# Input projection in seven block products, with tokens in three outer parts

## The chip, the cores and the metric

The kernel runs on one core of a Trainium2 chip. The core has a matrix engine (PE, TensorE), three engines for elementwise work (DVE or VectorE, ACT or ScalarE, POOL or GpSimd), a queue engine (SP) that here issues all transfers, and 16 DMA engines. The metric is the device time of one launch in microseconds (us). Before the change it is 1186.73 us, the median of three runs (1184.58 to 1187.98).

## The reference, cut to what matters

One layer with a pooling half and a recurrent half, 2048 prompt tokens and 8 sequences of 8 new tokens (2112 tokens in all), model width 1024. All is float32.

```python
xn = rms_norm(x, norm_pre)
z  = xn @ w_in                      # 1024 -> 4096: v_pool | g_pool | u_lru | g_lru, 1024 columns each
# pooling: causal mean over the last 2/4/8/16 tokens (by channel group) minus the token,
#          then a 256x256 map per group and a scale per channel
y_pool = (mean_window(v_pool) - v_pool) @ pool_w[g] * pool_scale
# recurrence: causal convolution of width 4, two sigmoid gates by 128x128 blocks, a scan
xs = conv4(u_lru) ; r = sigmoid(xs @ wa + ba) ; gi = sigmoid(xs @ wx + bx)
log_a = -8 * r * softplus(-lam) ; a = exp(log_a)
h_t = a_t * h_{t-1} + xs * gi * sqrt(max(-expm1(2*log_a), 1e-12))
merged = concat(y_pool * silu(g_pool), h * silu(g_lru)) @ w_out
y = x + rms_norm(merged, norm_post)  # and the new pool, conv and scan states
```

## The kernel before

Channels lie on the 128 partitions and tokens along the free axis. Each float32 operand of the matrix engine is split into a high and a low float32r half (`split`, L102 to L109: the high half by a copy on ACT, the low half by a subtraction on DVE or POOL), and each product is taken as three matmuls, high x high, high x low and low x high (`z_k`, L302 to L304; `mm3`, L316 to L318; `product`, L978 to L980).

The input projection has 32 blocks of 128 output channels: 8 value blocks and 8 gate blocks of the pooling half, 8 input blocks (u) and 8 gate blocks (lg) of the recurrent half. The tokens are cut into five chunks (four of 426 and one of 408). The split activations of all chunks stay in SBUF (`xn`), and the outer loop runs over blocks: a block's weight is loaded and split once and then meets all five chunks, at 8 x 3 matmuls for a chunk. There are these stages:

- A first stage in an order written out by hand (`tc.manual_schedule`): the first chunk, row norms from a second copy of x (L224), the normalisation of the other chunks (L272, L280, L289), and pooling group 0, with its map by `pool_mm`.
- Pooling groups 1 to 3. For these the map `pool_w` is multiplied into the weight beforehand (`fold_mm`, 12 foldings of 12 matmuls of 256 columns), so that only the last chunk, whose new states need the raw values, still goes through the map. Beside it `w_combos` (L452) forms differences of blocks of `w_out` for the last stage.
- The recurrent half: 40 steps (8 blocks x 5 chunks) in a hand-written order. A step has U's 24 matmuls, the convolution (`conv_stage`: one ACT pass and three DVE passes, L504), the split of its result, the gate matmuls of the step before, the gates (`lru_gates`, L537 to L541), the reciprocal of 1 + tanh on DVE (L1280), the scan (`lru_scan`, L545 to L554) and the product with silu of the gate (`lru_out` on POOL, L566). The decay a is 2/(1 + tanh(lam4 * r)) - 1.
- The output projection, which already takes seven products of 512 x 512 blocks for eight, 56 products of 24 matmuls of 512 columns for 16 x 128 token rows and a short one for the last 64 tokens. It reads the mixed activations back from DRAM (`mixed`) in tiles of 128 tokens.

Every engine works off its own instructions in order. Outside the hand-ordered parts a planner fixes the order when the kernel is built. All transfers are issued by SP in one queue, which stands still while a transfer waits for its tile.

## Time and profile before

| what | value |
|---|---|
| median of three runs | 1186.73 us |
| the profiled execution itself | 1187.95 us |
| its span, first to last instruction | 1186.1 us |
| mean granted TensorE clock | 0.996 |
| DMA moved | 146.93 MB, mean 124 GB/s |
| DVE reciprocals, L1280 | 40, 112.4 us |
| ACT table loads at L1292 and L1272 | 41, 52.6 us |

Busy time of an engine counts the time in which it had an instruction under way. For PE it is not the time at peak rate, since matmuls overlap: the mean of a matmul of 426 columns is 0.36 us, but the next one starts after about half of that. The rate is read from the distance of two starts.

### The profile page before, as it was taken

To read this page: it belongs to the slowest core of one execution; us is meant where nothing else is said; L and a number is where in the kernel's file an instruction comes from. 1 tells how busy PE (TensorE), PEld (TensorE's weight loads), DVE (VectorE), ACT (ScalarE), POOL (GpSimd) and SP (SyncE) were. 2 spreads that over 40 slices of the span, in tenths; PEclk is the share of its full clock that TensorE was granted. 3 is DMA by queue.
4 is the path that set the end of the run, shared out by engine and by line. 5 is a ranking of instruction groups with operands and counts; after the bars stand their busy time and mean duration, and the time that the engine had idled before them with its cause. 6 is when DMAs were issued, how large, how long until landed. Compare 5 with 4: busy or idle time off the path is not lost. (4 is left out here: it accounts for less than half of the span.)

```text
span 1186.1 us, 16264 instructions
## 1 busy us (share of the span) xinstructions
PE 1166.3 (98%) x5794; PEld 1075.2 (91%) x5794; DVE 827.9 (70%) x1201; ACT 551.5 (46%) x1015; POOL 356.4 (30%) x486
## 2 busy tenths in 40 slices
PE   7999999999999999999999999999999999999997
PEld 5899899999999999999999999999968888888886
DVE  4787344443625556888888888889876678888687
ACT  5753311221231136767676676767744333344232
POOL 4145402410431243333334433334310002221242
PEclk9999999999999999999999999999999999999999
DMA  9712533632630110110111111114479866777553
GB/s 341 268 60 62 184 129 115 189 118 75 201 95 30 65 52 26 45 45 33 45 41 54 49 45 45 33 41 120 133 206 259 243 177 189 229 209 232 166 166 142
DMA packets 127904, 146.93 MB, mean 124 GB/s; under 512 B 12432, under 2 KB 87440, under 8 KB 127824
## 3 DMA queue, kind: packets, MB, share of 16 engines
q1 hardware_dynamic: 127824, 145.91, 39.2%
q8 instruction: 45, 0.74, 0.3%
q14 instruction: 35, 0.29, 0.1%
HBM read 106.37 MB, written 39.24 MB: 123 GB/s over the span
## 5 line engine op out<-in xcount | busy, mean ns | idle before, releaser
L504 DVE SCALAR_TENSOR_TENSOR xs<-u,parT,xs 128x426 f32<-128x426 f32 (+1 forms) x120 | 109.2, 910 | 46.9 <-ACT xs L500 30.3
L302 PE MATMUL v<-xh,w 128*128 128x426 f32 (+2 forms) x320 | 116.0, 364 | 6.5 <-ACT w L595 5.6
L971 POOL TENSOR_TENSOR xr<-ac,xr 128x512 f32<-128x512 f32 x28 | 47.6, 1720 | 229.5 <-DMA s2d<-a 110.6
L303 PE MATMUL v<-xl,w 128*128 128x426 f32 (+2 forms) x320 | 115.5, 362 | 0.9 <-DVE xl L611 0.6
L302 PE MATMUL g<-xh,w 128*128 128x426 f32 (+1 forms) x320 | 114.7, 359 | 0.6 <-ACT w L106 0.6
L304 PE MATMUL g<-xh,w 128*128 128x426 f32 (+1 forms) x320 | 114.1, 357 | 0.7 <-POOL w L109 0.7
L304 PE MATMUL v<-xh,w 128*128 128x426 f32 (+2 forms) x320 | 114.1, 360 | 0.4 <-DVE w L109 0.4
L303 PE MATMUL g<-xl,w 128*128 128x426 f32 (+1 forms) x320 | 113.9, 356 | 0.0
L302 PE MATMUL u<-xh,w 128*128 128x426 f32 (+1 forms) x320 | 113.7, 355 | 0.0
L302 PE MATMUL lg<-xh,w 128*128 128x426 f32 (+1 forms) x320 | 113.7, 355 | 0.0
L304 PE MATMUL lg<-xh,w 128*128 128x426 f32 (+1 forms) x320 | 113.5, 355 | 0.0
L304 PE MATMUL u<-xh,w 128*128 128x426 f32 (+1 forms) x320 | 113.4, 354 | 0.0
L303 PE MATMUL lg<-xl,w 128*128 128x426 f32 (+1 forms) x320 | 113.4, 354 | 0.0
L303 PE MATMUL u<-xl,w 128*128 128x426 f32 (+1 forms) x320 | 113.2, 354 | 0.0
L1280 DVE RECIPROCAL rv<-rv 128x426 f32<-128x426 f32 (+1 forms) x40 | 112.4, 2811 | 0.0
L978 PE MATMUL p<-ws,s 128*128 128x512 f32 (+1 forms) x264 | 102.4, 388 | 0.0
L979 PE MATMUL p<-ws,s 128*128 128x512 f32 (+1 forms) x264 | 102.1, 387 | 0.2 <-DVE ws L109 0.2
L980 PE MATMUL p<-ws,s 128*128 128x512 f32 (+1 forms) x264 | 102.0, 387 | 0.1
L980 PE MATMUL p<-ws,a 128*128 128x512 f32 x192 | 75.8, 395 | 1.1 <-DVE a L109 1.1
L978 PE MATMUL p<-ws,a 128*128 128x512 f32 x192 | 75.7, 394 | 0.1
L979 PE MATMUL p<-ws,a 128*128 128x512 f32 x192 | 75.5, 393 | 0.0
L365 DVE TENSOR_TENSOR s<-e 128x440 f32<-128x440 f32 (+3 forms) x40 | 29.1, 728 | 65.4 <-ACT e L336 49.3
(225 smaller groups left out, 2803.2 us busy)
## 6 DMA issues: line engine op xcount, KB each, us to landing
a<-mixed SPq DMA_DIRECT2D x112, 256.0 KB, 4.3
wr<-in_w_in SPq DMA_DIRECT2D x56, 256.0 KB, 3.0
tok<-in_x SPq DMA_DIRECT2D x16, 512.0 KB, 10.2
wo<-in_w_out SPq DMA_DIRECT2D x32, 256.0 KB, 3.7
wtd<-wo SPq DMA_DIRECT2D x32, 256.0 KB, 2.4
w<-wtd SPq DMA_DIRECT2D x32, 256.0 KB, 3.9
xr<-in_x SPq DMA_DIRECT2D x32, 256.0 KB, 3.7
out<-xr SPq DMA_DIRECT2D x30, 256.0 KB, 2.7
```

What stands on the lines that cost most here:

```text
L302: nc.tensor.matmul(out, lhsT=wh, rhs=xh, start=(k == 0), stop=False)
L303: nc.tensor.matmul(out, lhsT=wh, rhs=xl, start=False, stop=False)
L304: nc.tensor.matmul(out, lhsT=wl, rhs=xh, start=False, stop=(k == KT - 1))
L365: nc.vector.tensor_tensor(out=dst[:, first:L], in0=src[:, first:L], in1=src[:, first - sh:L - sh], op=ALU.add)
L504: nc.vector.scalar_tensor_tensor(out=xs, in0=E[:, k:k + n], scalar=col(C_CW + 8 * k, b), in1=xs, op0=ALU.mult, op1=ALU.add)
L971: (eng or nc.vector).tensor_tensor(out=out, in0=a, in1=b, op=op)
L978: nc.tensor.matmul(out, lhsT=ah, rhs=wh, start=start and k == 0, stop=False)
L979: nc.tensor.matmul(out, lhsT=ah, rhs=wl, start=False, stop=False)
L980: nc.tensor.matmul(out, lhsT=al, rhs=wh, start=False, stop=stop and k == KT - 1)
L1280: nc.vector.reciprocal(out=v, in_=v)
```

## The change

The 32 blocks are taken in pairs (16 pairs) and the chunks in pairs too: six chunks of 352 tokens, in three parts of 704. For a pair of blocks, a pair of chunks and the two halves of the 1024 input channels, the 2 x 2 x 2 block product is done with seven products instead of eight (a "quad", `quad_slot`). Each product ("slot") has 4 x 3 matmuls of 352 columns. Four combinations of the four x quarters (T1 to T4) and four of the four weight quarters are formed by additions and split. Five PSUM sums per quad are put together by one ACT copy, one more ACT copy, and five DVE additions that read PSUM.

Tokens are outermost: all 16 pairs are run for part 0, then for part 1, then for part 2. The weight combinations are formed and split in part 0 (for V, G and U of the first pair in part 1, since these three are taken without combinations in part 0), stored to DRAM as split pairs of 512 KB (`wsd`), and loaded from there in parts 1 and 2, one for each slot, seven slots ahead. Of the seven low halves of a quad four are formed on POOL (`LO_POOL`) and three on DVE.

The whole input projection is one hand-ordered sequence. A loop over slots issues the matmuls of one slot, then what became due: evacuations of the slot before, one waiting small matmul group (a pooling map or a gate), delayed transfers, and steps of the generators (`pool_chain`, `conv_chain`, `lru_chain`, `x_chain`, `combos_chain`), as long as the costs written beside their `yield` fit a budget of 1.92 us for each of DVE, ACT and POOL (0.96 us more with a small matmul group).

The folding of `pool_w` into the weight is gone; all four groups of the pooling half go through the map. The reciprocal is gone: ACT gives a first value of 1 + a by Exp and the tanh of half the exponent, and one Newton step for 2/(1 + tanh) mends it, three DVE passes over 704 elements in place of the reciprocal and one pass. Sigmoids are formed with tanh. Elementwise work runs on 704 tokens at a time (728 with the states in the last part). The last stage is kept, with other buffers.

The diff, cut to its core:

```diff
-CW = 426
-CHUNKS = [(s, min(s + CW, T_ALL)) for s in range(0, T_ALL, CW)]
+CW = 352
+MW = 2 * CW
+NM = 3
+CHUNKS = [(s, s + CW) for s in range(0, T_ALL, CW)]
+AHEAD = 7
+SLOT = 1.92
+ORDER = (1, 6, 5, 7, 4, 2, 3)
+XOF = {1: "X11", 6: "T2", 5: "T1", 7: "T3", 4: "T4", 2: "X21", 3: "X22"}
...
+    def quad_product(out, t, name, start, stop, chain=False):
+        for k in range(HK):
+            wh, wl = w_parts(t, k)
+            xh, xl = (xq(name, k, i) for i in range(2))
+            mm(out, wh, xh, start and k == 0, False, chain)
+            mm(out, wh, xl, False, False, chain)
+            mm(out, wl, xh, False, stop and k == HK - 1, chain)
...
+    LO_POOL = (0, 3, 5, 6)
+
+    def w_step(n):
...
+        t = w_tiles[n] = half_tile(f"w{m}{kind}{p}_{i}")
+        if q not in PREP:
+            nc.sync.dma_start(out=flat, in_=wsd[:, key, :])
+            return 0.0, 0.0, 0.0
...
+        elif i == 1:
+            tadd(s1, r["21"], r["22"])
+            tsub(src, s1, r["11"])
+        elif i == 2:
+            tsub(r["21"], r["11"], r["21"])
+        elif i == 4:
+            tsub(s4, r["12"], r["s2"])
...
+        pool = i in LO_POOL
+        split(t[:, 0, :], t[:, 1, :], src, AC, G if pool else V)
+        if m < LM:
+            later(2, lambda: nc.sync.dma_start(out=wsd[:, key, :], in_=flat))
...
+        if pid == 1:
+            quad_product(bank("a"), w, name, True, True)
+
+            def evac():
+                t["tmp"] = t_tile(f"q{n}")
+                AC.copy(out=U(1), in_=t["a"])
+        elif pid == 6:
+            quad_product(bank("b"), w, name, True, True)
+
+            def evac():
+                tadd(U(0), t["b"], U(1))
...
+        elif pid == 7:
+            quad_product(bank("c"), w, name, True, True)
+
+            def evac():
+                tadd(U(1), t["c"], U(0))
+                put_sum(q, 1, 1, t["e"], U(1))
...
+        elif pid == 2:
+            quad_product(t["a"], w, name, False, True, True)
+
+            def evac():
+                AC.copy(out=dst_parts(q, 0, 0)[0][0], in_=t["a"])
...
-        nc.vector.reciprocal(out=v, in_=v)
+        AC.activation(out=gi, in_=gi, func=AF.Identity, bias=ones[:, 0:1])
+        G.tensor_tensor(out=gi, in0=gi, in1=v, op=ALU.mult)
+        AC.activation(out=v, in_=r, func=AF.Exp, scale=nlam[:, b:b + 1], bias=nlam[:, b:b + 1])
+        AC.activation(out=r, in_=r, func=AF.Tanh, scale=lam2[:, b:b + 1], bias=lam2[:, b:b + 1])
+        AC.activation(out=v, in_=v, func=AF.Identity, bias=ones[:, 0:1])
+        V.scalar_tensor_tensor(out=u, in0=r, scalar=1.0, in1=v, op0=ALU.add, op1=ALU.mult)
+        AC.activation(out=r, in_=r, func=AF.Sqrt)
+        V.scalar_tensor_tensor(out=u, in0=u, scalar=-4.0, in1=v, op0=ALU.add, op1=ALU.mult)
+        V.scalar_tensor_tensor(out=r, in0=r, scalar=-0.25, in1=u, op0=ALU.mult, op1=ALU.mult)
+        AC.activation(out=u, in_=u, func=AF.Identity, scale=-0.5, bias=neg1)
+        V.scalar_tensor_tensor(out=gi, in0=r, scalar=0.5e-6, in1=gi, op0=ALU.max, op1=ALU.mult)
+        V.tensor_tensor_scan(out=r, data0=u, data1=gi, initial=0.0 if m == 0 else hh[:, b:b + 1],
+                             op0=ALU.mult, op1=ALU.add)
...
+    def one_slot(pe_fn, used=(0.0, 0.0, 0.0), n_pe=1):
+        length = SLOT
+        outs = [pe_fn()] if pe_fn else []
+        for f in evacs:
+            f()
+        if pe_q and pe_q[0][0] <= now[0]:
+            outs.append(pe_q.pop(0)[1]())
+            length += 0.96
+        evacs.extend(o[0] for o in outs)
+        due_dmas()
+        bud = [min(length - u, length + c - u) for u, c in zip(used, carry)]
+        bud[0] -= sum(o[1] for o in outs)
+        run_gens(bud)
...
+        for n in range(7 * len(QUADS)):
+            qi, i = divmod(n, 7)
+            q = QUADS[qi]
+            if i == 0:
+                while t_free() < {"V": 1}.get(q[2], 3) or (q[2] == "V" and (e_free() < 2 or not sums_done(*q[:2]))):
+                    one_slot(None)
+                quad_begin(q)
...
+            tr = transition(ti) if ti >= 0 else used
+            ws = w_step(n + AHEAD)
+            one_slot(body, [a + b for a, b in zip(tr, ws)])
...
-T_BUFS = 9
+T_BUFS = 14
-E_BUFS = 4
+E_BUFS = 6
+W_BUFS = 8
```

`transition` forms the split x quarters of the next part in the last quad of a part and the first of the next: four quarter combinations and the low halves of T1 to T4 on DVE, the low halves of X11, X21 and X22 on POOL. The order of the quads in a part is V, G, L of the pair before, U, for four channel pairs each, and L of the last pair.

More of the change, by code (lines that the diff above doesn't have):

```diff
@@ L855, in hymba_kernel @@
     ol = late[:, 472:544].rearrange("p (b t) -> p b t", b=NH)
[L856 to L860 removed]
+    hp = sb.tile([P, NH, PB], F32, name="hp")
+    hu = sb.tile([P, NH, CB], F32, name="hu")
+    hh = sb.tile([P, NH], F32, name="hh")
+    lam2 = sb.tile([P, NH], F32, name="lam2")
+    nlam = sb.tile([P, NH], F32, name="nlam")
+    hb = sb.tile([P, 2, NH], F32, name="hb")
@@ new lines, in x_lo, with blocks, w_load_raw @@
+    def x_lo(name, src, eng):
+        hi = q3(name, 0).bitcast(F32)
+        if isinstance(src, list):
+            for o, i, h in zip(parts(q3(name, 1)), parts(src), parts(hi)):
+                tsub(o, i, h, eng)
+        else:
+            tsub(q3(name, 1), src, hi, eng)
+    def blocks(kind, p):
+        return [KINDS[kind] + 2 * p + j for j in range(2)]
+    def w_load_raw(blk, h, tile):
+        nc.sync.dma_start(out=tile, in_=w_in[blk, :, PIECE * h:PIECE * (h + 1)])
+        return tile
@@ L1018, in p1_out @@
     def p1_out(g):
[L1019 removed]
+        nc.scalar.copy(out=acc_new(("m", g)), in_=bank["a", g])
     def p1(g):
```

1759 lines of the change are left out of this document (918 added, 841 removed).

## The prediction

> **What bounds the kernel now.** I read the page's busy times first, then the table of stretches, because one share over the whole span mixes stages with different limits (columns: PE, weight load, DVE, ACT, POOL, each with its count, then clock, DMA share, GB/s).
>
> ```profile
> PE 1166.3 (98%) x5794; PEld 1075.2 (91%) x5794; DVE 827.9 (70%) x1201; ACT 551.5 (46%) x1015; POOL 356.4 (30%) x486
> ...
> 0.00:50.00 50.00, 40.76 (x178) 35.02 (x179) 27.10 (x55) 31.12 (x64) 13.65 (x35) 0.98 0.94 345
> ...
> 437.00:875.00 438.00, 437.69 (x2248) 422.02 (x2248) 363.54 (x402) 303.17 (x508) 162.06 (x266) 1.00 0.19 58
> 875.00:1179.00 304.00, 302.74 (x1325) 244.64 (x1323) 234.28 (x420) 112.15 (x241) 54.36 (x34) 1.00 0.71 207
> ```
>
> PE is occupied from the first matmul to the last; only the start (40.76 of 50 us) and the last 7 us have gaps. So matmul issue bounds the time, and the question is what each matmul costs and which engine follows PE. In the recurrent stage (437 to 875) DVE is at 83%. The price of a matmul is the distance of two starts, in the order of time on PE:
>
> ```profile
> 702.43 0.35 PE L302 MATMUL u<-xh,w 128*128 128x426 f32 x1
> ...
> 706.91 0.36 PE L304 MATMUL u<-xh,w 128*128 128x426 f32 x1
> ...
> 1004.52 0.39 PE L978 MATMUL p<-ws,a 128*128 128x512 f32 x1
> ...
> 1010.06 0.39 PE L978 MATMUL p<-ws,s 128*128 128x512 f32 x1
> ...
> 1173.05 0.28 PE L978 MATMUL p<-ws,s 128*128 128x256 f32 x1
> ...
> 1178.04 0.28 PE L978 MATMUL p<-ws,s 128*128 128x256 f32 x1
> ```
>
> There are 23, 24 and 42 distances between these: 0.195 us for 426 columns, 0.231 for 512, 0.119 for 256. On the line between them 352 columns cost 0.161 and 408 cost 0.185.
>
> **Part 1, matmuls.** The counts are from the code; the rows of before agree with it (two of the twelve input groups, a folding, a gate).
>
> ```profile
> L302 PE MATMUL v<-xh,w 128*128 128x426 f32 (+2 forms) x320 | 116.0, 364 | 6.5 <-ACT w L595 5.6
> L303 PE MATMUL u<-xl,w 128*128 128x426 f32 (+1 forms) x320 | 113.2, 354 | 0.0
> L318 PE MATMUL f<-pw,wtl 128*128 128x256 f32 x48 | 13.7, 286 | 0.2 <-POOL wtl L109 0.2
> L317 PE MATMUL i<-xl,lws 128*128 128x426 f32 x32 | 11.6, 361 | 0.0
> ```
>
> Before: input 32 blocks x 24 x (4 x 0.195 + 0.185) = 741 us; folding 144 x 0.119 = 17; maps 96 at 0.19 = 18; gates 240 x 0.195 = 47; together 823. After: 45 quads x 84 plus six blocks taken plainly, 288, is 4068 x 0.161 = 655; maps 288 x 0.161 = 46; gates 288, 47; together 748. **PE gains 75 us**, and if PE still set the pace the time would be near 1113. The output stage keeps its matmuls, so nothing there.
>
> **Part 2, what DVE and POOL must do beside it.**
>
> ```profile
> L1280 DVE RECIPROCAL rv<-rv 128x426 f32<-128x426 f32 (+1 forms) x40 | 112.4, 2811 | 0.0
> ```
>
> Removed are these 112 us of reciprocals. Added are two DVE passes per recurrent block, five PSUM additions per quad, the weight combinations and the x combinations. Most of the added passes read two tensors from SBUF, and the trace shows what such a pass does beside POOL:
>
> ```profile
> 998.53 3.42 POOL L971 TENSOR_TENSOR xr<-ac,xr 128x512 f32<-128x512 f32 x2 [6.48 <-DVE ac L1111]
> ...
> 999.03 1.78 DVE L109 TENSOR_TENSOR a<-a,a 128x512 fp32r<-128x512 f32 x1
> 1000.81 1.70 DVE L971 TENSOR_TENSOR a<-a,a 128x512 f32<-128x512 f32 x1
> 1002.43 0.68 DVE L109 TENSOR_TENSOR s<-a,s 128x512 fp32r<-128x512 f32 x1
> 1003.03 0.68 DVE L971 TENSOR_TENSOR a<-a,a 128x512 f32<-128x512 f32 x1
> ...
> 73.25 2.10 POOL L289 TENSOR_TENSOR xl<-xr,xh 128x852 fp32r<-128x852 f32 x1 [1.43 <-ACT xh L280]
> ...
> 73.36 2.36 DVE L272 SCALAR_TENSOR_TENSOR xr<-xr,parT,r 128x426 f32<-128x426 f32 x4
> ```
>
> While POOL runs two subtractions, DVE's passes take 1.78 and 1.70 us; right after, the same passes take 0.68 and start 0.60 apart. Two at 0.60 and two of POOL at 1.29 alone make 3.8, and the stretch took 4.0: one after the other. At 73 us DVE's passes have r in PSUM, and four take 2.36 us beside a POOL pass of the usual length: no loss. So DVE's two-SBUF passes and POOL's work share one resource, and their times add. [...]
>
> The prices, each as lowest, median and highest (ns) of a line's passes:
>
> ```profile
> L109 POOL TENSOR_TENSOR wtl<-wt,wth x12: 1284/1288/1300, 124.8 to 343.2; 128x512 fp32r<-128x512 f32 x12
> L566 POOL TENSOR_TENSOR lsg<-lsg,rv x32: 1100/1112/1126, 467.4 to 869.7; 128x426 f32<-128x426 f32 x32
> L289 POOL TENSOR_TENSOR xl<-xr,xh x6: 2025/2068/2385, 73.2 to 91.3; 128x852 fp32r<-128x852 f32 x6
> L548 DVE SCALAR_TENSOR_TENSOR tg<-rv,tg x40: 602/603/609, 465.4 to 873.0; 128x426 f32<-128x426 f32 x32, 128x432 f32<-128x432 f32 x8
> L554 DVE TENSOR_TENSOR_SCAN rv<-rv,hh,tg x32: 1103/1105/1120, 475.9 to 874.0; 128x426 f32<-128x426 f32 x24, 128x432 f32<-128x432 f32 x8
> L504 DVE SCALAR_TENSOR_TENSOR xs<-u,parT,xs x120: 654/665/1620, 438.2 to 848.8; 128x426 f32<-128x426 f32 x96, 128x432 f32<-128x432 f32 x24
> L106 ACT CAST w<-wr x56: 609/618/624, 139.9 to 796.0; 128x512 fp32r<-128x512 f32 x56
> ```
>
> By length: POOL 1.29 us for 512 elements, 1.71 for 704, 3.3 for 1408; DVE 0.60 for 512 from start to start, 0.80 for 704, 1.6 for a quarter, 1.68 for a scan of 704. The convolution's passes (L504) show the spread that POOL makes, 0.65 alone and up to 1.62.
>
> *Part 0 of the tokens* (13 quads): PE needs 13 x 84 x 0.161 + 192 small matmuls x 0.161 = 207 us. POOL: four weight halves for each of 13 quads that are prepared, 52 x 1.29 = 67; 27 passes of 704 (convolution and pooling splits, two products per recurrent block, of which some fall into part 1), 46; eight small splits, 10; two quarters, 6.5; some thirty copies at 0.2, 6: 136. DVE with two SBUF inputs: seven passes for each of 13 quads, 91 x 0.60 = 55; pooling 28 x 0.82 and edges, 26; convolution 21 x 0.80 = 17; recurrence 24 x 0.80 + 6 scans = 29; normalising and combining the next x, 16: 143. **Together 279 us on the shared resource against 207 of PE.** DVE's PSUM additions, 13 x 5 and 16 maps at 0.49, 39 us, may lie beside POOL, but each is shorter than a POOL pass, so I add 10 us for the rest that is lost; 13 us of recurrence can slip into the next part, as far as the 14 token tiles let it. Net +69. The bounds are 0 (everything of POOL lies beside PSUM additions and idle time) and +110 (nothing does). ACT, 13 x 7 x 0.62 = 56 for the weights and some 130 for the rest and its table loads, is near 190 of 207, no bound while the other pair is slower, but no reserve either. A w tile is made seven slots ahead, 13.5 us, and eight PSUM banks last about as many slots; so PE runs at the pace of DVE and POOL after that.
>
> *Part 1*: PE 247 us (16 quads, 16 maps, 16 gate groups). POOL 89 (32 passes of 704 and what slipped, two quads' weights, three quarters); DVE 140 (weights 8, pooling 23, convolution 22, recurrence 49, x 19, the differences of w_out 19): 229, plus 46 of PSUM additions that only DVE can do. Close to PE, with the work bunched at both ends: +14 (0 to +35). *Part 2*: 66 and 90 against 247: +0.
>
> **Part 3, transfers.** A tile of `wsd` is 0.524 MB. Part 0 stores 13 x 7 and moves some 79 MB; part 1 loads 91 of them, stores 21, and with x, `mixed` and `w_out` (8.4 in, 8.4 out) moves 94 MB in 247 us, 382 GB/s.
>
> ```profile
> 10.00:45.00 35.00, 33.00 (x154) 29.25 (x153) 18.85 (x31) 23.07 (x48) 9.70 (x12) 1.00 1.04 398
> ```
>
> That row moved 398 GB/s with all DMA engines taken, so part 1 stands at 96% of what the core has shown; I count nothing more than the +14 above, with up to +20 in the range. SP's queue stands still when a store waits for DVE or POOL, and the weight loads behind it wait too, with seven slots in reserve. [...]
>
> **Part 4, start and end.** Row norms now come after the second x chunk, softplus and twelve half squares, and no matmul but the six plain blocks can run before; I put 8 us of idle PE there and the first quad's T quarters, four combinations and four low halves at 1.6 on DVE, at some 10, together about 18 where the start of before lost 9: **+10** (0 to +20). At the end the last recurrent block's chain lies under 15 slots of output products: +2.
>
> **Sum**, from the profiled execution's own 1187.95 us (span 1186.1 and 1.85 around it, 1.2 above the median of the runs): -75 + 10 + 69 + 14 + 2 = +20, so 1208, and 1207 beside the median.
>
> **The rivals.** *A, PE keeps the pace* (the other side): POOL's passes fall beside DVE's PSUM additions and pauses, and recurrent work slips into parts 1 and 2, where DVE and POOL have room. Place: part 0; price: of the 83 us of parts 0 and 1 some 30 remain; it decides if less than 62 do. For it: in the recurrent stage of before POOL's L566 never met DVE (1100 to 1126 ns). Against: there DVE spent 112 us in reciprocals that read one tensor, which are gone. Time 1155, and 1125 if nothing remains. *B, transfers bind in part 1*: against the row above stores and loads are mixed and rows of w_out are short; +20 and a queue that holds the weights back, so 1230. *C, it does not do what it says*, since a weight load lasts 0.19 us (PEld 1075.2 / 5794) and a matmul of 352 columns would wait for it: 4644 x 0.186 = 862 in place of 748. The losses on DVE would mostly lie beside that, so near 1260. Against it are the 256-column matmuls, 0.119 apart with a load each.
>
> **How the numbers follow.** Forecast 0.55, A 0.28, B 0.15, C 0.02. The forecast's own range is 1180 to 1235, by the bounds of part 0 and the start. Two in ten are left out at 1140 (deep in A) and 1245. About 0.3% either way, 3.6 us, is what a measurement of this kernel tells from no change: faster is A and a little of the forecast's low end, 0.29; the same 0.05; slower 0.66.
>
> **What would show it.** DVE near 100% in part 0 with passes of two SBUF inputs at 1.5 us or more, POOL above 40% there, PE at about 75% of its slots, and PE nearly full in part 2: right. PE full in part 0, with DVE's passes near their lowest, is A. PE waiting for `w<-wsd` in part 1, with DMA above 0.95, is B. Matmuls of 352 columns more than 0.17 apart without a wait would be C. The sum is wrong if deferred work or a bunched start moves more than 30 us between parts.

## The result, and the profile after

The changed kernel takes 1341.84 us (median of four runs, 1339.65 to 1345.97) where the kernel before took 1185.65 us beside it (1184.35 to 1187.98). The ratio is 1.132, with a 95% interval of 1.129 to 1.135. The prediction was 1207 us, in a range of 1180 to 1235: the direction was right, the size was not. The profiled execution has a span of 1337.9 us, 151.8 more than the 1186.1 of before.

The first two lines are from the page of after, the busy times and the granted clock in 40 slices. Then come the stretches of after between the starts of the parts (columns: length; busy time with count of PE, weight load, DVE, ACT, POOL; granted clock, DMA share, GB/s). They are the start, the first quad, the rest of part 0, part 1, part 2, and the output stage with what is left of part 2.

```profile
PE 1152.4 (86%) x6118; PEld 1069.0 (80%) x6118; DVE 990.3 (74%) x1370; ACT 645.8 (48%) x1031; POOL 463.9 (35%) x408
...
PEclk9979779868878899989899979999988999999998
```

```profile
0.00:63.51 63.51, 55.11 (x302) 51.96 (x303) 48.26 (x98) 28.08 (x63) 24.24 (x40) 1.00 0.49 171
63.51:102.45 38.94, 20.07 (x87) 18.34 (x85) 37.37 (x42) 18.99 (x27) 23.59 (x12) 0.76 0.60 221
102.45:391.05 288.60, 212.14 (x1168) 206.81 (x1167) 238.77 (x265) 159.47 (x248) 151.37 (x110) 0.85 0.67 247
391.05:691.74 300.69, 267.51 (x1576) 264.40 (x1576) 218.25 (x259) 155.58 (x222) 99.50 (x88) 0.94 0.83 299
691.74:967.41 275.67, 257.22 (x1545) 254.87 (x1545) 185.82 (x250) 144.63 (x197) 101.54 (x121) 0.96 0.78 270
967.41:1337.90 370.49, 340.35 (x1450) 272.65 (x1449) 261.85 (x459) 139.01 (x277) 63.64 (x39) 0.96 0.64 188
```

Two things stand against the kernel before. PE is idle for 185.5 us in place of 19.8. And it is busy for 1152.4 us in place of 1166.3, a fall of 14 where the work was to fall by 75. The slots are full of the same matmuls, but the granted clock, the third column from the end, is 0.76 to 0.96 in the three parts. So there are two losses, pauses (166 us more) and slow matmuls (61 us more than the work), and together with the 75 they make the 152.

The list of PE's waits of after says for what it paused (in all, times, longest). Bank e is the PSUM bank in which products 5 and 3 of a quad accumulate.

```profile
PE e L236 <- DVE g L861: 71.2, 14, 11.6
PE e L236 <- DVE e L861: 18.0, 4, 8.0
PE y L238 <- ACT pw L129: 14.9, 1, 14.9
PE e L236 <- DVE u L861: 14.0, 5, 4.2
PE a L236 <- ACT q L882: 11.0, 4, 7.6
PE p L442 <- ACT s L129: 8.7, 1, 8.7
```

Line 236 is the matmul that accumulates in a bank that holds something already. Product 3 adds into bank e, so it must wait until DVE has read product 5 out of it (L861), which belongs to the evacuation of product 7, two slots earlier. These waits for bank e are 71.2 + 18.0 + 14.0 = 103 us, 60 of them in part 0, 29 in part 1 and 14 in part 2. One of them, in the order of time, on each engine of after:

```profile
369.85 2.08 PE L238 MATMUL c<-XN,w0L 128*128 128x352 f32 x12
371.77 2.08 PE L238 MATMUL d<-XN,w0L 128*128 128x352 f32 x12
373.69 2.08 PE L236 MATMUL a<-XN,w0L 128*128 128x352 f32 x12
387.36 3.89 PE L236 MATMUL e<-XN,w0L 128*128 128x352 f32 x12 [11.59 <-DVE g L861]
```

```profile
373.06 3.30 DVE L132 TENSOR_TENSOR w1V<-s2V,w1V 128x512 fp32r<-128x512 f32 x1 [3.09 <-ACT w1V L129]
...
378.72 0.51 DVE L310 TENSOR_TENSOR q<-b,q 128x352 f32<-128x352 f32 x1
379.16 1.68 DVE L307 TENSOR_TENSOR XA<-XA 128x704 f32<-128x704 f32 x2
...
386.24 0.51 DVE L310 TENSOR_TENSOR q<-c,q 128x352 f32<-128x352 f32 x1
386.79 0.52 DVE L861 TENSOR_TENSOR g<-e,q 128x352 f32<-128x352 f32 x1
```

```profile
372.59 3.23 POOL L307 TENSOR_TENSOR XN<-XA,XN 128x1408 fp32r<-128x1408 f32 x1 [0.21 <-DMA wsd<-w0L]
```

Bank c was full at 371.9 us. DVE added it up only at 386.2, behind the passes written ahead of the sum: it had stood 3.1 us for a cast of ACT (until 373.1), then a weight low took 3.30 us (0.68 for the one at 378.12, with no POOL pass beside it) beside a POOL pass of 3.23, and eleven more passes came before the sum. PE did the two products that it could, d and a, and stood for 11.6 us. The product after the pause took 3.89 us in place of 2.08.

### The profile page after: what moved, and what is told of

Its sections match the earlier page's. It is cut to its first block, busy times and chain, and to the rows that moved or that the text cites. A ratio compares the mean times of both kernels' runs of the same rounds, so it can differ in the third digit from the quotient of the medians.

```text
span 1337.9 us, 17719 instructions
## 1 busy us (share of the span) xinstructions
PE 1152.4 (86%) x6118; PEld 1069.0 (80%) x6118; DVE 990.3 (74%) x1370; ACT 645.8 (48%) x1031; POOL 463.9 (35%) x408
## 5 line engine op out<-in xcount | busy, mean ns | idle before, releaser
L442 PE MATMUL p<-XN,s 128*128 128x512 f32 (+1 forms) x224 | 88.3, 394 | 8.9 <-ACT s L129 8.7
L1059 DVE SCALAR_TENSOR_TENSOR xs<-u,parT,xs 128x704 f32<-128x704 f32 (+1 forms) x72 | 88.3, 1227 | 3.8 <-ACT xs L1049 2.6
L444 PE MATMUL p<-XN,s 128*128 128x512 f32 (+1 forms) x224 | 88.0, 393 | 2.0 <-DVE s L132 2.0
L443 PE MATMUL p<-XN,s 128*128 128x512 f32 (+1 forms) x224 | 88.2, 394 | 0.4 <-DVE XN L132 0.2
L1100 POOL TENSOR_TENSOR ig<-ig,xs 128x704 f32<-128x704 f32 (+1 forms) x24 | 46.2, 1927 | 94.7 <-ACT ig L1099 80.6
L238 PE MATMUL y<-dh,pw 128*128 128x352 f32 x192 | 56.5, 339 | 15.5 <-ACT pw L129 14.9
L307 POOL TENSOR_TENSOR xl<-xs,xh 128x704 fp32r<-128x704 f32 (+1 forms) x24 | 45.6, 1902 | 66.6 <-ACT xh L1064 53.4
L435 DVE TENSOR_TENSOR a<-a,a 128x512 f32<-128x512 f32 x48 | 34.0, 714 | 37.0 <-DMA a<-mixed 32.4
L238 PE MATMUL z<-XN,w 128*128 128x352 f32 x288 | 53.3, 347 | 7.4 <-ACT w L1316 5.4
L442 PEld LDWEIGHTS p<-XN,s 128*128 128x128 f32 x224 | 43.0, 192 | 19.3 <-ACT s L129 9.1
L238 PEld LDWEIGHTS z<-XN,w 128*128 128x128 f32 x288 | 49.9, 203 | 10.3 <-ACT w L1316 5.4
L444 PE MATMUL p<-XN,a 128*128 128x512 f32 x137 | 54.3, 396 | 0.1
L442 PE MATMUL p<-XN,a 128*128 128x512 f32 x137 | 54.2, 396 | 0.0
L443 PE MATMUL p<-XN,a 128*128 128x512 f32 x137 | 54.2, 395 | 0.0
L444 PEld LDWEIGHTS p<-XN,s 128*128 128x128 f32 x224 | 42.9, 191 | 12.2 <-DVE s L132 2.7
L443 PEld LDWEIGHTS p<-XN,s 128*128 128x128 f32 x224 | 43.0, 192 | 10.7 <-DVE XN L132 1.1
```

Source lines behind the costliest of these rows:

```text
L238: nc.tensor.matmul(out, lhsT=lhsT, rhs=rhs, start=start, stop=stop)
L307: (eng or V).tensor_tensor(out=out, in0=a, in1=b, op=ALU.subtract)
L435: (eng or nc.vector).tensor_tensor(out=out, in0=a, in1=b, op=op)
L442: nc.tensor.matmul(out, lhsT=ah, rhs=wh, start=start and k == 0, stop=False)
L443: nc.tensor.matmul(out, lhsT=ah, rhs=wl, start=False, stop=False)
L444: nc.tensor.matmul(out, lhsT=al, rhs=wh, start=False, stop=stop and k == KT - 1)
```

## The experiments

Eighteen runs, all of them variants of the changed kernel. The theories are named in the expectations: **coupling** (PE stands because banks e and a are needed again a few slots after they were filled, so that every delay on DVE or ACT beyond that stops PE), **shared path** (DVE's passes with two SBUF inputs and POOL's work exclude one another, and the sum of their times sets the pace), and **ordering** (the code writes slots without a product, where a quad waits for free tiles).

| run | median us | ratio to before, 95% |
|---|---|---|
| bank_apart | 1280.22 | 1.078 to 1.083 |
| low_dve | 1353.76 | 1.139 to 1.147 |
| ready_w | 1224.47 | 1.031 to 1.035 |
| pool_memset | 1246.73 | 1.050 to 1.055 |
| wide_budget | 1338.12 | 1.126 to 1.129 |
| apart_wide | 1293.42 | 1.089 to 1.092 |
| apart_memset | 1195.92 | 1.007 to 1.010 |
| recip | 1324.26 | 1.114 to 1.118 |
| apart_low_dve | 1310.76 | 1.102 to 1.107 |
| apart_recip | 1292.55 | 1.087 to 1.091 |
| apart_swap | 1288.89 | 1.082 to 1.088 |
| apart_recip_prods | 1294.98 | 1.089 to 1.093 |
| apart_no_taps | 1256.02 | 1.055 to 1.061 |
| apart_ready | 1179.43 | 0.990 to 0.995 |
| floor | 1146.11 | 0.963 to 0.968 |
| paused | 1329.91 (one run) | |
| apart_end | 1281.12 | 1.079 to 1.084 |
| apart_low_wide | 1315.86 | 1.108 to 1.112 |

### Product 3 in a bank of its own

```diff
 elif pid == 7:
     tadd(U(1), t["c"], U(0))
     put_sum(q, 1, 1, t["e"], U(1))
+    put_sum(q, 0, 1, t["e"], U(0))
...
 else:   # pid 3
-    quad_product(t["e"], w, name, False, True, True)
-        put_sum(q, 0, 1, t["e"], U(0))
+    quad_product(bank("f"), w, name, True, True)
+        for out, lo, hi, is8 in dst_parts(q, 0, 1):
+            f_ = t["f"][:, lo:hi]
+            tadd(out, as8(f_) if is8 else f_, out)
...
-return evac, {6: 0.5, 7: 1.0, 4: 0.5, 3: 0.5}.get(pid, 0.0)
+return evac, {6: 0.5, 7: 1.5, 4: 0.5, 3: 0.5}.get(pid, 0.0)
```

The last line tells the planner of the longer evacuation.

> Product 3 gets a PSUM bank of its own; the old bank e is summed into both of its destinations right after product 7, and product 3 is added to its destination afterwards (one more DVE pass of 352 columns a quad, 45 quads by 0.55 us = 25 us of DVE). The coupling theory (PE stands because products 3 and 2 accumulate into banks that DVE and ACT must read first, only two slots earlier) expects the 103 us that PE waited for bank e to go for the most part: 1240 to 1290 us. The shared-path theory (DVE's passes with two SBUF inputs and POOL's passes exclude one another, and their sum sets the pace) expects PE to stand at another bank instead, and the extra passes to be paid: 1330 to 1365 us.

1280.22 us: 61.6 us gone, although DVE has 53 instructions more (x1370 to x1423). The coupling theory's range, 1240 to 1290 us, holds it. The stretches of bank_apart, the rest of part 0 and parts 1 and 2:

```profile
96.66:364.33 267.67, 214.36 (x1191) 208.14 (x1191) 241.04 (x281) 156.44 (x246) 150.96 (x110) 0.87 0.73 269
364.33:642.67 278.34, 258.70 (x1552) 254.16 (x1551) 220.28 (x276) 159.31 (x227) 106.70 (x88) 0.96 0.88 322
642.67:909.36 266.69, 253.55 (x1539) 250.63 (x1538) 194.71 (x280) 147.54 (x198) 100.35 (x121) 0.97 0.81 286
```

DVE's busy time in part 0 is what it was (241 for 239 us), and the stretch is 21 us shorter. So it wasn't DVE's amount of work that was cut, but its lateness that was tolerated. Not all of it: the next wait in the line is that for bank a, where product 2 adds to product 1 and ACT must have copied it, 29.8 us in bank_apart where it was 11.0.

### The weight lows on DVE

```diff
-LO_POOL = (0, 3, 5, 6)
+LO_POOL = ()
```

> All seven low halves of a quad's weights on DVE instead of four of them on POOL: in part 0 some 64 POOL passes of 1.55 us go and as many DVE passes of 0.7 us come. The shared-path theory expects their sum to fall by 64 x 0.85 = 54 us and the time by 20 to 50 us: 1290 to 1320 us. The coupling theory (what counts is how late DVE's own queue reaches the sums that free PE's banks) expects DVE's 45 us more to be paid in part 0: 1350 to 1390 us.

1353.76 us, 12 more than after. The shared-path theory as the prediction had it, a sum of two times, expected 20 to 50 less than after. POOL's busy time fell by 111 us and DVE's by 9 (from 990.3 to 981.3) although DVE had 64 passes more, so its passes did become shorter; the time rose all the same. The rise doesn't lie where the passes were moved: part 0 is 3 us shorter (324.4 for 327.5), though DVE's and POOL's busy times there fell by 96 us together, part 1 is 9 longer, and part 2 and the end, where no weights are made, 4 and 5. PE's waits for bank e are 86.6 us, fewer than the 103 of after, those for bank a 20.8 in place of 11.0, and the planner also writes more slots without a product (39 in place of 27). So this run speaks against the sum as a pace, and doesn't show that DVE's passes were paid.

### Ready weights

In `w_step`, quads after the first load the seven stored tiles of the first quad. The weight combinations, splits, raw loads and stores are left out, and the weights are not those of the quads.

```diff
-if q not in PREP:
-    nc.sync.dma_start(out=flat, in_=wsd[:, key, :])
+if q != PREP[0]:
+    nc.sync.dma_start(out=flat, in_=wsd[:, (KINDS[kind0] // 8 * NG + p0) * 7 + i, :])
```

> Every quad after the first loads seven ready weight tiles from the store (those of the first quad, so the weights are the wrong ones); the weight combinations, splits, raw loads and stores of part 0 are left out. The prediction's step (weight preparation on DVE and POOL is what holds part 0, at +79 us over PE) expects part 0 to fall from 327 us to some 220 to 250 us, parts 1 and 2 unchanged to 10 us: 1235 to 1265 us. If part 0 is held by something else (first quad, the rounds of x, ACT), it falls by less than 40 us: over 1300 us.

1224.47 us, 117 less and below the expected range, since part 1 gains too. The stretches of ready_w from the first quad to the end of part 2:

```profile
63.79:95.72 31.93, 18.75 (x85) 17.34 (x85) 30.61 (x35) 16.94 (x22) 19.72 (x9) 0.73 0.61 228
95.72:290.52 194.80, 190.90 (x1193) 189.99 (x1192) 141.47 (x188) 110.69 (x160) 69.53 (x65) 1.00 0.88 310
290.52:570.32 279.80, 257.76 (x1551) 255.54 (x1551) 195.86 (x242) 149.37 (x209) 85.69 (x76) 0.96 0.89 314
570.32:850.05 279.73, 257.32 (x1545) 254.99 (x1545) 185.92 (x247) 144.94 (x197) 101.56 (x121) 0.96 0.76 262
```

Part 0 falls from 327.5 to 226.7 us, and its rest is at PE's pace at full clock: that the preparation of the weights holds part 0 was right. The edit takes away DVE's and POOL's passes together with ACT's casts and the transfers, so it doesn't tell which of them it was. Part 1, which prepares three more quads, falls by 21, more than expected. Part 2 stays, and its loss of some 30 us has nothing to do with preparing weights.

### POOL without reads

POOL's two-input passes (weight lows, X lows, lows before maps and gates, the products of the recurrence) become fills of the same outputs; these subtractions and products are left out.

```diff
-tsub(xl, xs, xh.bitcast(F32), G)
+G.memset(xl.bitcast(F32), 0.0)
```

> POOL's two-input passes (weight lows, X lows, the lows before the maps and gates, the products of the recurrence chain) are replaced by fills of the same output without a read from SBUF; those subtractions and products are left out. The shared-path theory expects DVE's passes to lose their long cases and the parts to come close to PE's pace: 1230 to 1280 us. The coupling theory alone (DVE's order and the two-slot distance, whatever POOL does) expects 1310 to 1340 us.

1246.73 us, 95 less. DVE's convolution passes, in the groups by line, first of after and then of pool_memset (count, busy us, mean ns, idle before):

```profile
L1059 DVE SCALAR_TENSOR_TENSOR xs<-u,parT,xs 128x704 f32<-128x704 f32 (+1 forms) x72 | 88.3, 1227 | 3.8 <-ACT xs L1049 2.6
```

```profile
L1063 DVE SCALAR_TENSOR_TENSOR xs<-u,parT,xs 128x704 f32<-128x704 f32 (+1 forms) x72 | 70.5, 981 | 3.7 <-ACT xs L1053 1.5 <-issue 1.0
```

The same 72 instructions lose a fifth, and DVE as a whole 132 us (990.3 to 857.9). So POOL's two-input passes do make DVE's longer, here 1227 for 981 ns, and the kernel gains in all three parts: part 0 falls by 54 us, part 1 by 24, part 2 by 16. The fills are shorter than the passes that they replace (POOL's busy time falls from 463.9 to 243.2 us), so a share of the 95 us may come from POOL's own results being there earlier.

### Do the two losses add up?

> Product 3 in a bank of its own, and POOL's two-input passes replaced by fills (those subtractions and products are left out). Alone the two brought 61 and 95 us. If coupling and shared path are two separate losses, they add up: 1342 - 156 = 1186 us (1180 to 1205). If DVE's lateness, which POOL causes, is what PE sees at bank e, the second removes mostly what the first had removed already: 1220 to 1245 us.

Both edits together: 1195.92 us, 146 less, where the two alone had brought 62 and 95. So they are nearly separate, as the first expectation had it. A reading that fits, not tested further: POOL makes DVE late, the bank decides how much lateness PE bears, and there is enough of both left for each. The stretches of apart_memset, rest of part 0, part 1, part 2:

```profile
91.66:317.28 225.62, 201.75 (x1192) 196.81 (x1191) 183.05 (x283) 159.28 (x249) 60.71 (x112) 0.95 0.85 321
317.28:577.69 260.41, 252.53 (x1552) 249.85 (x1551) 185.18 (x272) 157.31 (x223) 41.31 (x88) 0.99 0.94 341
577.69:826.48 248.79, 247.71 (x1540) 246.89 (x1539) 170.76 (x278) 146.59 (x197) 49.69 (x119) 1.00 0.85 307
```

Part 2 is at PE's pace, 248.8 us, of which PE is busy 247.7. That is the 247 of the prediction.

### The written order

```diff
-bud = [min(length - u, length + c - u) for u, c in zip(used, carry)]
+bud = [min(1.3 * length - u, 1.3 * length + c - u) for u, c in zip(used, carry)]
```

> The kernel after with one number changed: each slot's allowance of DVE, ACT and POOL work is 1.3 times a slot's length. The order that the code writes then holds 4 slots without a product in place of 27 (quads that wait for free tiles or for pooling sums), and the pooling, gate and recurrence passes come earlier on DVE's queue. If the empty slots are the loss (the ordering theory), some 23 slots by 1.9 us go: 1285 to 1310 us. If the coupling theory holds, DVE's queue is longer ahead of the sums that free bank e, and the waits for it grow by as much as the empty slots shrink: 1330 to 1380 us.

> Both: product 3 in a bank of its own and the allowance of 1.3 slots. With the two-slot distance gone, the coupling theory expects DVE's longer queue to be borne by the banks that are left, so that the empty slots' 23 x 1.9 us are gained on top: 1235 to 1260 us. The shared-path theory (DVE and POOL have no more throughput) expects no gain over the 1280 us of the bank alone: 1270 to 1300 us.

1338.12 and 1293.42 us: 4 less than after, and 13 more than bank_apart. The ordering theory falls. With fewer slots without a product PE stands at banks instead (waits for bank e 74.4 + 24.6 + 18.6 = 118 us in wide_budget, for bank a 38.1 in apart_wide), and its idle time in wide_budget is 185.0 us, as in after. The second run, though, lies in the range that the shared-path theory gave; the gain that the coupling theory expected there did not come.

The number of slots without a product changes with most edits, since the planner goes by the costs written in the code: 27 in after, 29 in bank_apart, 4 and 5 in these two, 39 in low_dve, 33 in recip, 39 in apart_recip and 52 in apart_recip_prods.

### Weight lows once more

> Product 3 in a bank of its own, and all seven weight lows on DVE (64 POOL passes of some 1.6 us to 64 DVE passes of 0.7). On DVE's own coupling to PE the move alone cost 12 us. If that was the two-slot distance, the shared path's shorter sum now shows: 1245 to 1270 us. If DVE's total (241 of 268 us in part 0) is the bound whatever frees the banks, it costs again: 1285 to 1305 us.

> As apart_wide (1293 us: own bank, allowance of 1.3 slots), with all seven weight lows on DVE. POOL has 64 passes of some 1.6 us less, DVE 64 of 0.7 us more; the written order holds 11 slots without a product against 5. If the shared path's sum sets the pace, it falls by 54 us and the time to 1245 to 1280 us. If DVE's own queue does, 1298 to 1325 us.

1310.76 and 1315.86 us, 31 and 22 more than the kernels without this edit, the first above both of its ranges. It mixes two things, since the planner, which counts DVE's budget, also writes 41 slots without a product in place of 29; the second keeps them at 11 against 5. The rest of part 0 of apart_low_wide:

```profile
97.58:393.80 296.22, 218.03 (x1192) 209.51 (x1191) 235.63 (x326) 154.56 (x242) 67.21 (x63) 0.88 0.67 244
```

DVE and POOL together are busy for 303 us there, where they were 385 in the same stretch of apart_wide (236.44 and 148.16), and the stretch is 11 us longer. A smaller sum on the shared path was no gain. As a rule for the pace the sum is refuted; that POOL's two-input passes make DVE's longer (1227 ns in after, 981 in pool_memset) is not. Why the move costs is shown only in part: in apart_low_dve the waits for bank a grew from 29.8 to 61.1 us, as much as the time, but in apart_low_wide they are 34.9 where apart_wide has 38.1, and the largest new waits are single ones before maps (10.8 us until a short instruction of POOL, 7.2 until one of ACT).

### The Newton step undone

```diff
-AC.activation(out=v, in_=r, func=AF.Exp, ...)
...
-V.scalar_tensor_tensor(out=u, in0=r, scalar=1.0, in1=v, op0=ALU.add, op1=ALU.mult)
-V.scalar_tensor_tensor(out=u, in0=u, scalar=-4.0, in1=v, op0=ALU.add, op1=ALU.mult)
+AC.activation(out=v, in_=r, func=AF.Identity, bias=ones[:, 0:1])
+V.reciprocal(out=v, in_=v)
```

> The decay by a reciprocal again in place of the Newton step: per recurrent block and part one DVE reciprocal of 704 elements (4.6 us by the length of the one in the kernel before) for two two-input passes of 0.8 to 1.0 us, and one exponential less on ACT; 24 times, so DVE +65 us, shared path -40 us. The coupling theory expects DVE's long pass ahead of the sums to cost PE: 1355 to 1400 us. The shared-path theory expects little, since POOL runs beside a pass that reads one tensor: 1325 to 1355 us.

> Product 3 in a bank of its own, and the decay by a reciprocal. The reciprocal alone brought 18 us. If that is a gain of the shared path (POOL works beside a pass that reads one tensor), it adds to the bank's 61: 1255 to 1268 us. If it came from the order of the sums for bank e only, it is gone here: 1275 to 1300 us.

> As apart_recip, and the two products of the recurrence chain (48 passes of 704, on POOL 1.9 us each) on DVE (0.8 us alone). POOL loses some 80 us, DVE gains some 40, the shared path loses 40 us, of which a third or so falls into each part. The shared-path theory expects 15 to 35 us less than apart_recip: 1225 to 1250 us. If DVE's own total is the bound, it costs 5 to 25 us: 1265 to 1290 us.

The reciprocal alone gives 1324.26 us, 18 less, where the lower expectation began at 1325; with the bank 1292.55, which is 12 more than bank_apart and in the range given for a gain at bank e only. DVE is busier with it (990.3 to 1031.8 us), ACT less (645.8 to 607.1). That range does not show the cause, since another wait moved: the one for ACT's cast of `pw`, the weight of the pooling map, which comes and goes with the order of ACT's queue. After has one such wait of 14.9 us, recip none, and bank_apart 3.6 us of them. Apart_recip has 23.3 us in two cases, and apart_recip_prods 49.9 us in three.

The waits for bank e fell by 11 us in recip (103 to 93). In part 2, where nothing waits for `pw`, the reciprocal gains 15 us without the bank and still 6 with it (275.7 to 261.1, 266.7 to 260.5). So as the kernel stands the Newton step is no gain; whether it is one with the bank, these runs don't tell.

Moving the two products of the recurrence from POOL to DVE on top (L1100 and L1134, `G.tensor_tensor` to `V.tensor_tensor`) gives 1294.98 us, no less than apart_recip and above both ranges: parts 1 and 2 gain 24 and 7 us (285.9 to 262.0, 260.5 to 253.9), and the first quad and the rest of part 0 lose 33. Some 6 us of that are small matmuls that move from part 1 into part 0 (36 at 0.16), and 27 us are the longer waits for `pw`, all of them in part 0. So the shared path pays in the later parts; in part 0 the loss came by ACT's cast, and that DVE's own amount of work was the reason is not shown.

### Products 3 and 2 exchanged

```diff
-ORDER = (1, 6, 5, 7, 4, 2, 3)
+ORDER = (1, 6, 5, 7, 4, 3, 2)
...
```

The last two weight quarters and x quarters are made in the new order too.

> Product 3 in a bank of its own and before product 2, which accumulates into bank a: ACT's copy of bank a has four slots in place of three before PE needs it. PE waited 29.8 us for that copy with product 3's own bank. The coupling theory expects 15 to 30 us of it to go: 1250 to 1268 us. If ACT is late for a reason that one slot doesn't cover, or DVE and POOL set the pace: 1272 to 1285 us.

1288.89 us, 9 more than bank_apart and above both ranges. Bank a is now needed five slots after product 1 has been done in place of four (the expectation counted one less in both). The wait for it fell as expected, 29.8 to 15.4 us, but a wait for the cast of `pw` by ACT came up, 20.9 us in two cases. Giving one bank more time moved the stop to another thing that ACT makes.

### DVE relieved

The three passes of the convolution (L1059) are left out and the other instructions stay; their taps are not added.

```diff
-V.scalar_tensor_tensor(out=xs, in0=E[:, k:k + n], scalar=col(C_CW + 8 * k, b), in1=xs, ...)
 yield 1.0, 0, 0, 0
```

> Product 3 in a bank of its own, and the 72 convolution passes on DVE left out (the taps other than the last one are not added); POOL, ACT, PE and the written order are the same. DVE loses 70 to 88 us, some 23 in part 0, 29 in parts 1 and 2 each. If DVE's total is what is left in parts 0 and 1, the time falls by 30 to 50 us: 1230 to 1250 us. If the order of hand-offs (ACT's copy of bank a, the empty slots) is what is left: 1262 to 1282 us.

1256.02 us, 24 less than bank_apart, for 90 us less of DVE (996.7 to 906.6). It lies between the two expectations: of each us taken off DVE about a quarter is gained, so its amount of work is a part of what is left, and not the most of it.

### No preparation, own bank, and no reads by POOL

> Product 3 in a bank of its own, and ready weight tiles after the first quad (combinations, splits, raw loads and stores of weights left out; the weights are those of the first quad). Alone the two brought 61 and 117 us. In part 0 without preparation nothing waited for bank e any more, so only the bank's gain in parts 1 and 2 (22 and 9 us) adds: 1185 to 1200 us. Full addition would be 1164 us.

> All three: own bank, POOL's two-input passes as fills, ready weight tiles (weight preparation and POOL's subtractions and products are left out). If the 75 us of PE work are really saved, PE is near its pace from the second quad to the last: 63 + 28 + 195 + 249 + 248 + 367 = 1150 us (1140 to 1165). If the block products lose time on PE that the stages so far hide, over 1175 us.

1179.43 us, a little under the first expectation, and 1146.11 us, within the second. The stretches of floor, from the first quad to the end of part 2:

```profile
64.52:86.02 21.50, 16.03 (x87) 15.07 (x86) 21.24 (x28) 12.59 (x16) 7.17 (x4) 0.84 0.80 299
86.02:276.03 190.01, 190.01 (x1191) 190.01 (x1191) 132.38 (x207) 113.07 (x164) 34.23 (x66) 1.00 0.91 317
276.03:524.74 248.71, 248.37 (x1551) 247.85 (x1551) 174.97 (x256) 150.07 (x210) 36.50 (x78) 1.00 0.94 345
524.74:776.53 251.79, 248.89 (x1539) 248.32 (x1538) 169.77 (x276) 146.66 (x197) 49.28 (x119) 0.99 0.85 301
```

This is what the change had to offer: PE's busy time is 1098.3 us, 68 less than before, and the kernel is 3.5% faster than before. It leaves out work that has to be done, so it is no version to use. With the bank and without the preparation of weights, but with POOL's passes (apart_ready), the kernel is at 0.992 of before. Part 1 moves 345 GB/s here and PE is busy for 248.4 of 248.7 us.

### The clock

Two dummy matmuls in each quad of part 2 of apart_memset (they write a bank that the product overwrites), and between them 0 to 48 fills on POOL that the second one waits for.

```diff
+if q[0] == LM:
+    mm(bank("c"), dly, xq(name, 0, 0), True, True)
     quad_product(t["c"], w, name, True, True)
+    for _ in range(PAUSE[...]):
+        G.memset(dly.bitcast(F32), 0.0)
...
+if q[0] == LM:
+    mm(bank("d"), dly, xq(name, 0, 0), True, True)
     quad_product(t["d"], w, name, True, True)
```

> As apart_memset (part 2: PE busy 247.7 of 248.8 us, clock 1.00), with two dummy matmuls in each quad of part 2 and between them 0 to 48 short fills on POOL that the second one waits for: pauses of PE from nothing to some 7 us, all else the same. If the granted clock falls after pauses, the products behind the long pauses show matmuls 0.3 us apart in place of 0.161, and PE's busy time in part 2 grows by 10 to 30 us over the 253 us that the dummies make. If the clock falls for another reason (DVE's or DMA's load), PE's busy time stays within 3 us of 253.

Part 2 of paused has PE busy for 280.6 us, 28 over the 253. Rows of PE in paused, at four of the pauses:

```profile
658.20 0.66 PE L239 MATMUL d<-XN,dly 128*128 128x352 f32 x1 [4.81 <-POOL dly L907]
658.66 3.72 PE L239 MATMUL d<-XN,w2V 128*128 128x352 f32 x12
662.18 2.60 PE L237 MATMUL a<-XN,w2V 128*128 128x352 f32 x12
...
773.60 0.66 PE L239 MATMUL d<-XN,dly 128*128 128x352 f32 x1 [12.87 <-POOL dly L907]
774.05 3.72 PE L239 MATMUL d<-XN,w2V 128*128 128x352 f32 x12
777.57 2.90 PE L237 MATMUL a<-XN,w2V 128*128 128x352 f32 x12
...
809.30 0.43 PE L239 MATMUL d<-XN,dly 128*128 128x352 f32 x1 [1.29 <-POOL dly L907]
809.57 2.09 PE L239 MATMUL d<-XN,w2L 128*128 128x352 f32 x12
...
827.43 0.66 PE L239 MATMUL d<-XN,dly 128*128 128x352 f32 x1 [4.09 <-POOL dly L907]
827.89 3.31 PE L239 MATMUL d<-XN,w2U 128*128 128x352 f32 x12
831.04 2.08 PE L237 MATMUL a<-XN,w2U 128*128 128x352 f32 x12
```

After 1.29 us of pause twelve matmuls took 2.09 us, where they take 2.08 without one. After 4.09 us and more they took 3.3 to 3.7 us, and in some cases part of the next twelve was slow too (2.60 and 2.90 us in place of 2.08); after 12.87 us it was hardly worse than after 4.81. The granted clock of the part is 0.86, where apart_memset has 1.00. The list of waits has 103.6 us for the dummy in 14 cases, one of 1.29 us and 13 of 4.09 to 13.83, so these 13 pauses brought on average about 28 / 13 = 2 us of slow matmuls each. DVE and ACT are as busy as without the dummies (171.5 and 146.7 us), and POOL's fills stand before the short pause as before the long ones, so the pauses do it. Between 1.29 and 4.09 us this run has no case, but after has waits of that length before twelve matmuls: they take 2.18 to 2.21 us after waits of 1.35 and 1.75, 3.30 after 2.14, 3.74 after 2.71, again 2.19 after 3.23, and 3.89 after 4.04. Counted over the traces of after and all its variants, wherever twelve matmuls follow a wait and the twelve before it were at full speed: of 44 waits of 0.5 to 1.8 us none brought slow matmuls, of 45 of 1.9 to 3.3 us 28 did, and of 90 longer ones all.

### The end

In the last part of the tokens the stores of the recurrence's results are issued by POOL, so that the loads for the output stage don't stand behind them on SP's queue.

```diff
-nc.sync.dma_start(out=mixed[:, 8 + b, ...], in_=sg[:, :MW])
+(nc.gpsimd if m == LM else nc.sync).dma_start(out=mixed[:, 8 + b, ...], in_=sg[:, :MW])
```

> As bank_apart, and in the last part of the tokens the stores of the recurrence's results are issued by POOL, which makes them, in place of SP. If the eight weight loads behind the last of these stores on SP's queue are what the first p7 product waits for (8.6 us, then some 3 us at half clock), the end shrinks by 6 to 12 us: 1268 to 1275 us. If the wait comes from ACT's and DVE's splits or from the recurrence itself: 1277 to 1283 us.

1281.12 us, the same as bank_apart. SP does issue eight loads of `wtd` earlier (from 921.8 us on, where bank_apart issues them from 941.7 on), but six of their casts stand on ACT behind copies of output products. These two rows of ACT in apart_end show it:

```profile
946.33 0.58 ACT L483 COPY ac<-p 128x512 f32<-128x512 f32 x1 [4.49 <-PE p L238]
946.81 3.22 ACT L129 CAST XN<-w 128x512 fp32r<-128x512 f32 x6
```

So the stores on SP's queue were not the cause. That ACT's order is, these rows suggest; it was not tried.

## Why the prediction was wrong, step by step

**Part 1, matmuls: right.** Three starts of twelve matmuls in after are 1.92 us apart (369.85, 371.77, 373.69), 0.160 for one where 0.161 was forecast. Floor's PE time is 1098.3 us; 1166.3 - 75 makes 1091. The rest is slow matmuls, most of them in the output stage (a granted clock of 0.97 over 340.7 us of PE's busy time). Rival C falls by the same rows.

**Part 2, the size of DVE's and POOL's work: its fit is luck.** 279 us on the shared resource and 10 more, less 13 that slip, was the forecast for part 0. DVE was busy for 37.4 + 238.8 = 276 us there, but this time holds what DVE's passes lose beside POOL's (1227 for 981 ns in the convolution) and its additions from PSUM, and not POOL's work. POOL was busy for 23.6 + 151.4 = 175 us where 136 were counted: its weight lows took 1.5 to 2.1 us in the mean in place of the 1.29 of before. DVE in part 0 of pool_memset, where most of POOL's passes read nothing, was busy for 207 us; less the 39 that the prediction gives for PSUM additions and maps that makes 168 (an estimate) where 143 were counted.

**Part 2, the step that failed**: "A w tile is made seven slots ahead, 13.5 us, and eight PSUM banks last about as many slots; so PE runs at the pace of DVE and POOL after that." The number of banks isn't the distance. Products 3 and 2 accumulate in banks that have to be read out first, and so PE can be ahead of DVE's sums by two slots, 3.8 us, and of ACT's copy by four slots. The example at 373 us shows DVE 14.3 us late at bank c; the eight slots of 1.92 us that the prediction counted on would just have covered that. So part 0 doesn't run at DVE's pace, but stops whenever DVE is late and lets DVE and ACT wait in turn: 327.5 us for 276 of DVE, 84% and not near 100%. The forecast for it was 207 + 69 = 276, and 10 for the first quad, which has its share of the start: 286. Releasing bank e alone brought 62 us, and this was not due to less work, since DVE had more.

**The sum of two times as a rule for the pace: wrong**, too. Low halves on DVE make the sum shorter and the time longer (low_dve, apart_low_dve, apart_low_wide; in low_dve part 0 gains 3 us for 96 of the sum). What counts at bank e is what stands in DVE's queue ahead of a sum, as the example shows. POOL's reads are one cause of it: without them the kernel is 95 us shorter, of which POOL's shorter passes may be a share, and in part 2, where the prediction had put nothing ("66 and 90 against 247"), that brings back 16 of the 29 us lost. An engine with room on average was taken for an engine without effect.

**A term that was missing: the clock.** The rows show slow matmuls behind pauses (in after the twelve at 387.36 start 0.31 us apart in place of 0.16), and floor and after differ by 1152.4 - 1098.3 = 54 us of PE's busy time for the same matmuls. In paused, twelve matmuls took 2.09 us after a pause of 1.29 us and 3.31 to 3.73 after 4.09 and more, and the slow stretch lasted from 3.6 us (827.43 to 831.04) to 5.8 (691.41 to 697.21). After waits of 1.9 to 3.3 us both came: slow matmuls in 28 of 45 cases. Each wait that the prediction counted, in part 0 above all, should have had some 2 us added where it lasts 4.09 us or more.

**Part 3, transfers: right as far as tested.** PE's waits in after name no transfer, so rival B falls for the kernel as it is. At PE's full pace part 1 of floor moves 345 GB/s, but with loads in place of the 21 weight stores of that part; with the stores apart_memset moves 341 GB/s over 260 us, also without a wait of PE for a transfer in that part. The 382 GB/s of the forecast were reached in neither. No run shows the +20 that rival B adds: part 1 of apart_memset took 260.4 us, where 247 were counted for PE.

**Part 4: start right, end mis-sized.** PE was idle for 8.4 us up to the first quad (8 forecast). The first quad took 38.9 us where 13.5 of matmuls and 10 were counted; it takes 21.5 in floor. The end was put at +2. It loses some 22 us more in after (what is left of the 152 when the parts are taken off: 15 in the first quad, 26 in the rest of part 0, 40 in part 1 and 29 in part 2, beyond the 20 that were forecast), and the stretch is 366 to 375 us in every run, floor included. So it is a loss of its own. Its likely place is the wait of 8.7 us for ACT's `s` and the smaller ones beside it, with the slow matmuls behind them (a granted clock of 0.96 in the stretch); the cause stays open.

**Rival A** (PE keeps pace) asked whether POOL's passes fall beside DVE's pauses; they don't (the convolution's passes on DVE took 1227 ns in after and 981 in pool_memset). But the time that it gave for no loss at all in parts 0 and 1, 1125, is 21 us below floor, which is about the end.

What stays open: how the 84 us between bank_apart and apart_memset divide into shorter DVE passes and POOL's own results coming earlier (in bank_apart PE waits 9.7 us for POOL's `dl` and 9.2 for `xl`), what the weight lows on DVE cost in the order of the kernel with the bank, and how much the reciprocal is worth apart from the waits for `pw`.

## What to carry to other kernels

Where products accumulate in place, count how many slots lie between the evacuation that a bank waits for and the next product into it; that distance, not the number of banks, is the lateness that PE can bear, and a bank of one's own may be worth more than the DVE pass it costs (here two slots, 3.8 us, at bank e, and 61.6 us less for 53 DVE instructions more). Moving elementwise passes to the engine that frees PE's banks can cost time even if the two engines' total gets shorter: here 12 to 31 us where the sum promised a gain. An edit that moves costs also moves the written order, so look at every wait of PE before a gain or a loss is put down to one of them. And a wait of PE can have a second price: here slow matmuls came after all 90 waits of more than 3.3 us and after 28 of 45 of 1.9 to 3.3 us, some 2 us of them for each of the 13 long pauses of paused.

## What the runs showed of the hardware

The clock after a pause was the surprise: in paused the loss hardly grew with the length, since the twelve matmuls took 3.72 us after a pause of 4.81 us and 3.72 after one of 12.87, and the next twelve 2.60 and 2.90. In after, a weight low on DVE took 3.30 us beside one pass of POOL of 3.23 where another took 0.68 alone, and filling in place of reading on POOL took 132 us from DVE's busy time, although POOL still wrote the same tiles.
